# Indices and row weights on ScalarE, ranks ahead of splits, and another order at the end of an expert layer

## The chip, the cores and the metric

One core of a Trainium2 chip runs the whole program; there is no second core to wait for. The metric is the device time of one execution in microseconds (us), less is better. The engines run side by side, each through its own queue in order: TensorE (PE: matmuls, with weight loads listed apart as PEld), VectorE (DVE), ScalarE (ACT), GpSimd (POOL) and SyncE (SP), which here issues most of the DMA transfers. An instruction that waits holds back all that stands behind it on its engine.

## The reference

One decoder layer for 1024 tokens of width 1024:

```python
proj = x @ w_in + b_in                       # [q | k | v | u | g]
mix  = concat(attn(q, k, v), sgu(u, g)) @ w_out + b_out
h    = LN(alpha * x + mix)
y    = LN(alpha * h + MoE(h))
# MoE(h), top 4 of 32 experts for each token:
logits = h @ w_router + b_router
gates  = softmax(top_k(logits, 4))
gt  = minimum(rows @ w_gate[e] + b_gate[e], 7.0)
up  = clip(rows @ w_up[e] + b_up[e], -7.0, 7.0)
hid = gt * sigmoid(1.702 * gt) * (up + 1.0)
out = out.at[row_tok].add((hid @ w_down[e] + b_down[e]) * row_gate)
```

`rows` are the tokens that chose expert `e`, about 128 on average; each expert has three weight matrices of 1024 x 1024 in float32.

## The kernel before, in words

**Ahead of the experts.** Attention, gating, the output projection, the first layer norm and the router go block by block (eight blocks of 128 tokens). For each block `norm3a`/`norm3b` write `h`, split into two fp16 parts, to the table `htab` in DRAM, from which token rows are gathered later; they also write `h` to `h32` and `alpha * h` (scaled on GpSimd, L578) to the accumulator `acc`. `route1` to `route5` and their pieces (`route4a`, `route4p`, `route4g`) give each block its four experts, its gates and its place within each expert's list. The order of these calls, written out by hand for the last blocks, sets the order on every engine. The first two experts' token rows are found early: `places` makes one-hot rows, `rows` multiplies them with token numbers and gathers, and `early_g` and `weights_of` give those rows' gate weights from a tile `VE`.

**The expert loop.** `moe()` runs over 192 parts, called pieces: the two 512-column halves of gate ("g"), up ("u") and down ("d") of each of 32 experts. A piece is 96 matmuls (L1115): its 512 columns in four, 8 slices of the inner dimension, and three products of fp16 parts of weights and rows. The weights come as 1 MB halves into seven buffers `raw`. ScalarE makes the high fp16 part (`hi`, L948) and VectorE the low one (`lo`, L952), into one of three buffers `wsp`. So each piece costs two `hi` and two `lo`. Step `i` of the loop multiplies piece `i`, finishes piece `i-1` and splits the weights of piece `i+2`; the table `SEQ` gives the order within a step.

**The rows of an expert.** `rank` sorts the experts by load, in three parts between which other work is put (`next(rank)`); its result is the placement `PP` and a tile `V` with, for each token, its number and its gate weight for each slot. Expert slot `j` has a fixed room `CAP[j]` (88 to 256 rows; 48 groups of up to 128 rows for slots 2 to 31 and after). For each, events at fixed steps do `onehot` (VectorE, L1072), `rows_of` (TensorE, `V` times one-hot, L1082), `index` (one ScalarE copy, L932, and three GpSimd operations, L934 to L937, giving the token index `ix` and the weight `gw`), `gather` (GpSimd, indirect DMA `xg<-htab,ix`, L942), `xpose` (TensorE transposes, L1101) and `xcopy`. After the down pieces, `turn` transposes back and `combine` multiplies by `gw` (ScalarE) and adds to `acc` (indirect DMA).

**The end.** The eight blocks of `acc` are loaded back; the last expert's rows are added in SBUF apart. `FIN` says in which of the last steps each block's statistics (`s0` to `s7`, ScalarE and a power on GpSimd), its two passes (`a0` to `a7`, VectorE, L1327 and L1328, and a store L1329) and the last expert's end (`c1`, `c2`) are written. `c1` weights the last rows, adds, and takes their statistics with VectorE; `c2` normalizes and scatters them into the output, after all stores. `flags` checks all splits for numbers that are not finite and all experts for overflow. Every engine then reads that flag and skips a rescue path.

Of the kernel before, what the change touches and what calls it, by code (L numbers as in the profile page):

```python
# [20 lines left out]
EPS = 1e-5  # L21
# [10 lines left out]
FIN = {-3: ["s0", "s1", "a0"], -2: ["s2", "s3", "a1", "a2"], -1: ["s4", "s5", "a3", "a4"], 0: ["s6", "s7", "a5"],  # L32
       1: ["c1", "a6", "a7", "c2"]}
# [21 lines left out]
class Layer:  # L55
# [441 lines left out]
    def blocks(self):  # L497
# [112 lines left out]
        def route3a(b):  # L610
# [6 lines left out]
            gt = pb.tile([128, 44], F32, name="gt", bufs=2)  # L617
# [3 lines left out]
        def route3b(b):  # L621
# [4 lines left out]
            mr = pb.tile([128, 36], F32, name="mr", bufs=2)  # L626
# [39 lines left out]

        def early_g(b):
            sk = TK[b]
            for k in range(2):
                nc.vector.tensor_tensor(self.prod[:, k], sk[:, None, 32 + 32 * k:64 + 32 * k].to_broadcast([128, 2, NE]), self.SR,  # L670
                                        op=OP.mult)
            with nc.allow_low_precision(reason="one term of each sum differs from zero"):
                for k in range(2):
                    nc.vector.tensor_reduce(self.VE[:, b, :, 2 + k], self.prod[:, k], axis=AX.X, op=OP.add)
# [92 lines left out]
        norm3b(b - 1)  # L767
        self.loads(5)
# [3 lines left out]
        route1(b, (0,))  # L772
        norm3a(b)
        route1(b, (1,))
        route3b(b - 1)
        self.places(0, b - 2)
        route4p(b - 2)
        early_p(b - 2)
        route4g(b - 2)
# [3 lines left out]
        norm3b(b)  # L783
        route4p(b - 1)
        early_p(b - 1)
        self.places(b - 2, b)
        route3a(b)
        route3b(b)
        route4a(b)
        route4p(b)  # L790
# [4 lines left out]
        self.rows(1)  # L795
        self.loads()
# [120 lines left out]
    def weights_of(self):  # L917
        nc, p = self.nc, self.praw
        for j in range(2):
            self.rows_mm(j, 2)  # L920
# [678 lines left out]
```

## Time and profile before

| | |
|---|---|
| runs, us | 1731.23, 1731.42, 1733.17 (median 1731.42) |
| the profiled execution, us | 1732.75, its span 1731.0 |
| busy: PE | 1615.3 us (93%), 21936 instructions |
| busy: DVE | 1455.0 us (84%), 2128 |
| busy: ACT | 1184.8 us (68%), 1512 |
| busy: POOL | 509.4 us (29%), 437 |
| mean granted TensorE clock | 0.968 |

The span is the profiled part of one execution and its own time is 1.75 us longer. A busy share is a mean over stretches with different limits, so what an engine is worth is read for a stretch. In the rows below a timeline row is a start, a duration, the engine, the source line, the operation, what is written and what is read, its shape, and in brackets how long the engine stood idle before it and what released it. `x96` is a run of as many instructions. In the table of stretches each engine has its busy time and, behind it in brackets, its instructions; PEclk is the clock that TensorE was granted, as a share of full speed (2.4 GHz).

### The profile page before, as it was taken

How to read it: one execution, taken by the hardware profiler on the slowest of the kernel's cores; microseconds unless marked ns; L12 is line 12 of the kernel's file. 1: busy time of each engine (PE TensorE's matmuls, PEld its weight loads, DVE VectorE, ACT ScalarE, POOL GpSimd, SP SyncE). 2: the span in 40 equal slices, each digit the busy share in tenths (PEclk: the TensorE clock that was granted, in tenths of full speed). 3: DMA queues.
4: the chain of work that ended last, by engine and by line, in shares of the span. 5: the costliest groups of instructions: out<-in, count | busy, mean ns of one | idle time of the engine just before them, and what ended most of it. 6: DMA issues, size and time to landing. Idle time of an engine off the chain costs nothing. (4 is left out here: it accounts for less than half of the span.)

```text
span 1731.0 us, 51104 instructions
## 1 busy us (share of the span) xinstructions
PE 1615.3 (93%) x21936; PEld 1519.1 (88%) x21936; DVE 1455.0 (84%) x2128; ACT 1184.8 (68%) x1512; POOL 509.4 (29%) x437
## 2 busy tenths in 40 slices
PE   8989899946799999999999999999999999999981
PEld 7878666636799999999999999999999999999981
DVE  4555788898698898888898889898999989898886
ACT  4344455545677677777777777878787888777873
POOL 3310433332250712071215213222504142212013
PEclk9989999967899999999999999999999999999996
DMA  7331422279599998999999999999999999999993
GB/s 270 96 110 37 161 98 98 98 272 345 213 340 348 332 333 315 330 336 334 316 342 351 340 349 337 356 343 363 343 355 353 359 360 349 364 364 343 357 343 124
DMA packets 86713, 501.12 MB, mean 289 GB/s; under 512 B 14208, under 2 KB 14224, under 8 KB 37328
## 3 DMA queue, kind: packets, MB, share of 16 engines
q1 hardware_dynamic: 73632, 452.92, 69.8%
q0 software_dynamic: 12848, 44.86, 10.1%
q8 instruction: 174, 2.85, 0.6%
q14 instruction: 59, 0.48, 0.1%
HBM read 459.14 MB, written 38.60 MB: 288 GB/s over the span
## 5 line engine op out<-in xcount | busy, mean ns | idle before, releaser
L1115 PEld LDWEIGHTS <-wsp 128*128 128x128 f16 x18432 | 1161.1, 98 | 22.4 <-ACT xg L1323 6.5
L952 DVE SCALAR_TENSOR_TENSOR wsp<-raw,wsp 128x2048 f16<-128x2048 f32 x384 | 868.3, 2287 | 131.5 <-ACT wsp L948 129.7
L948 ACT ACTIVATE wsp<-raw 128x2048 f16<-128x2048 f32 x384 | 717.8, 1913 | 23.2 <-PE pu L1115 18.4
L1115 PE MATMUL pd<-hid,wsp 128*128 128x96 f16 (+30 forms) x6144 | 399.5, 227 | 10.2 <-ACT xg L1323 6.5
L1115 PE MATMUL pg<-xt,wsp 128*128 128x96 f16 (+30 forms) x6144 | 401.8, 227 | 0.0
L1115 PE MATMUL pu<-xt,wsp 128*128 128x96 f16 (+30 forms) x6144 | 398.7, 227 | 0.0
L1200 POOL DMA_INDIRECT acc<-y,ix x49 | 91.9, 1875 | 600.1 <-ACT y L1198 384.1
L934 POOL TENSOR_SCALAR ixf<-ixf,dummy 128x1 f32<-128x1 f32 (+7 forms) x48 | 118.1, 2461 | 272.1 <-ACT ixf L932 272.0
L1141 ACT ACTIVATE gv<-pg,bi 128x96 f32<-128x96 f32 (+30 forms) x256 | 79.9, 382 | 96.5 <-PE pg L1115 88.6
L942 POOL DMA_INDIRECT xg<-htab,ix x50 | 105.6, 2112 | 15.7 <-issue 12.1
L1198 ACT ACTIVATE y<-pt,gw 128x512 f32<-128x512 f32 (+7 forms) x98 | 62.0, 685 | 47.6 <-PE pt L1192 44.9
L1106 ACT COPY xt<-pt 128x1024 f16<-128x1024 f16 (+29 forms) x99 | 72.2, 783 | 31.0 <-PE pt L1101 15.8
L1169 ACT ACTIVATE hid<-uv 128x384 f16<-128x384 f32 (+28 forms) x102 | 47.7, 499 | 41.6 <-DVE uv L1166 41.6
L175 DVE TENSOR_TENSOR wl<-rw,wh 128x512 fp32r<-128x512 f32 x56 | 38.6, 737 | 40.7 <-ACT wh L174 40.7
L194 PE MATMUL psp<-xh,wh 128*128 128x512 f32 x160 | 65.4, 409 | 6.9 <-ACT xh L185 6.9
L195 PE MATMUL psp<-xl,wh 128*128 128x512 f32 x160 | 65.2, 407 | 3.8 <-DVE xl L187 3.7
L1101 PE MATMUL pt<-iden,xg 128*128 128x128 f16 (+29 forms) x800 | 46.2, 207 | 24.1 <-DMA xg<-htab,ix 16.7
L196 PE MATMUL psp<-xh,wl 128*128 128x512 f32 x160 | 64.4, 402 | 0.0
L1101 PEld LDWEIGHTS <-xg 128*128 128x128 f16 (+29 forms) x800 | 40.3, 99 | 26.4 <-DMA xg<-htab,ix 17.0
L523 PE MATMUL psp<-woh,mh 128*128 128x512 f32 x128 | 54.8, 428 | 3.5 <-issue 3.5
L1155 ACT ACTIVATE gv<-gv 128x384 f32<-128x384 f32 (+28 forms) x102 | 47.9, 515 | 11.4 <-DVE gv L1152 11.3
L1143 DVE SCALAR_TENSOR_TENSOR uv<-pu,bi 128x384 f32<-128x384 f32 (+28 forms) x102 | 53.7, 527 | 2.2 <-PE pu L1115 2.2
(278 smaller groups left out, 1746.5 us busy)
## 6 DMA issues: line engine op xcount, KB each, us to landing
raw<-w_g SPq DMA_DIRECT2D x128, 1024.0 KB, 7.7
raw<-w_u SPq DMA_DIRECT2D x128, 1024.0 KB, 7.4
raw<-w_d SPq DMA_DIRECT2D x128, 1024.0 KB, 7.1
rw<-w_t SPq DMA_DIRECT2D x20, 512.0 KB, 4.4
rw<-x_t SPq DMA_DIRECT2D x8, 512.0 KB, 4.6
rw<-w_m SPq DMA_DIRECT2D x8, 512.0 KB, 5.5
xb<-x SPq DMA_DIRECT2D x8, 512.0 KB, 4.3
htab<-t4k SPq DMA_DIRECT2D x8, 512.0 KB, 2.6
```

The source lines that it names most:

```text
L194: nc.tensor.matmul(pt, wh[:, k], xh[h, k], start=(k == 0), stop=False)
L195: nc.tensor.matmul(pt, wh[:, k], xl[h, k], start=False, stop=False)
L196: nc.tensor.matmul(pt, wl[:, k], xh[h, k], start=False, stop=(k == 7))
L934: v.tensor_scalar(t[:m, 0:1], t[:m, 1:2], self.dummy[:m, 1:2], t[:m, 0:1], op0=OP.mult, op1=OP.add)
L942: self.nc.gpsimd.indirect_dma_start(out=x[:m], out_offset=None, in_=self.htab, in_offset=bass.IndirectOffsetOnAxis(ap=self.IDX[j, o][:m], ...
L948: self.nc.scalar.activation(self.W[i][:, 0, 4 * z:4 * z + 4], self.RAW[i, z], AF.Copy, scale=WS)
L952: self.nc.vector.scalar_tensor_tensor(t[:, 1], self.RAW.pop((i, z)), WS, t[:, 0], op0=OP.mult, op1=OP.subtract, accum_out=self.FL[:, self. ...
L1101: nc.tensor.transpose(pt[:, k, :m], x[:m, z * D + 128 * k:z * D + 128 * k + 128], self.iden16[:m, :m])
L1106: (nc.vector.tensor_copy if j == 0 and z else nc.scalar.copy)(XT[j][:, z, :, o:o + m], XP.pop((j, o, z))[:, :, :m])
L1115: nc.tensor.matmul(out, w[:, wz, k, 128 * fc:128 * fc + 128], x[:, xz, k], start=(n == 0), stop=(n == 23))
L1141: nc.scalar.activation(out[:, q], src[:, q], AF.Identity, scale=1.0 / (HS * WS), bias=bi[:, c + q:c + q + 1])
L1200: nc.gpsimd.indirect_dma_start(out=self.acc, out_offset=bass.IndirectOffsetOnAxis(ap=IDX[j, o][:m], axis=0), in_=y[:m], in_offset=None, co ...
```

## The change

The change has five parts.

1. `index` no longer uses GpSimd: two ScalarE activations make the token index from the sums in PSUM, and a new `weight` makes the row weight with two more. Four ScalarE operations for a group take the place of one.
2. The two later parts of `rank` run at steps -4 and -1 instead of -1 and 1. For experts 2 and 3, `onehot` and `rows_of` run at steps 0 and 1, `index` and `gather` at 1 and 2, instead of steps 1 to 4 and 4 to 7.
3. `V` holds the token number and a one only once, the copies into it go from VectorE to ScalarE, `VE` and `early_g` are gone, and the row weights of the first two experts are made at step 4. Table constants come by a small DMA.
4. Ahead of the experts, `htab` is written first for the last two blocks, and `h32`, `alpha * h` (on ScalarE for these blocks) and `acc` follow later in `keep_h`; the first `hi` splits move up, the first `lo` splits into step -4.
5. At the end `FIN` has another order, the last statistics are made by ScalarE (`sums`), the flags stand after everything else, and the first half of the last down part goes through four slices of the inner dimension for both its groups before the other four.

```diff
-FIN = {-3: ["s0", "s1", "a0"], -2: ["s2", "s3", "a1", "a2"], -1: ["s4", "s5", "a3", "a4"], 0: ["s6", "s7", "a5"],
-       1: ["c1", "a6", "a7", "c2"]}
+FIN = {-3: ["s0", "s1"], -2: ["s2"], -1: ["s3", "a0", "a1"], 0: ["a2"],
+       1: ["c1", "s4", "s5", "a3", "s6", "a4", "c2", "s7", "a5", "a6", "a7", "c3"]}
...
+        def keep_h(b):
...
+            if b < NB - 2:
+                nc.gpsimd.tensor_scalar(ha, h, ALPHA, None, op0=OP.mult)
+            else:
+                nc.scalar.mul(ha, h, ALPHA)
             nc.sync.dma_start(self.acc[rows], ha)
...
         self.rows(1)
+        keep_h(b - 1)
+        self.loads(5)
+        keep_h(b)
+        self.hi(0, 1)
+        for z in range(2):
+            self.hi(1, z)
         self.loads()
         for i in (b - 2, b - 1, b):
-            if i > b - 2:
-                route4g(i)
-            early_g(i)
+            route4g(i)
             route5(i)
-        self.weights_of()
-        for z in range(2):
-            self.hi(0, z)
-            self.lo(0, z)
-            self.loads()
-        for z in range(2):
-            self.hi(1, z)
...
+    def weight(self, j, o, m, src):
         nc, p = self.nc, self.praw
+        t = p.tile([128, 4], F32, name="ixf", bufs=4)
+        nc.scalar.copy(t[:m, 2:3], src[:m, 2:3])
+        gw = self.GW[j, o] = p.tile([128, 1], F32, name="gw", bufs=16)
+        nc.scalar.activation(gw[:m], src[:m, 3:4], AF.Identity, scale=1.0 / G2S, bias=t[:m, 2:3])
 
     def index(self, j, o, m, src):
         nc, p = self.nc, self.praw
-        v = nc.gpsimd
         t = p.tile([128, 4], F32, name="ixf", bufs=4)
-        nc.scalar.copy(t[:m], src)
         ix = self.IDX[j, o] = p.tile([128, 1], I32, name="ix", bufs=16)
-        v.tensor_scalar(t[:m, 0:1], t[:m, 1:2], self.dummy[:m, 1:2], t[:m, 0:1], op0=OP.mult, op1=OP.add)
-        v.tensor_scalar(ix[:m], t[:m, 0:1], self.dummy[:m, 0:1], None, op0=OP.add)
-        gw = self.GW[j, o] = p.tile([128, 1], F32, name="gw", bufs=16)
-        v.tensor_scalar(gw[:m], t[:m, 3:4], 1.0 / G2S, t[:m, 2:3], op0=OP.mult, op1=OP.add)
+        nc.scalar.activation(t[:m, 0:1], src[:m, 0:1], AF.Identity, bias=self.dummy[:m, 0:1])
+        nc.scalar.activation(ix[:m], src[:m, 1:2], AF.Identity, scale=self.dummy[:m, 1:2], bias=t[:m, 0:1])
...
-                nc.vector.tensor_copy(self.V[:, 4 * g:4 * g + 4, :, 2 + i], pv[:, :, 32 + 32 * i:64 + 32 * i])
+                nc.scalar.copy(self.V[:, 4 * g:4 * g + 4, 1:, i], pv[:, :, 32 + 32 * i:64 + 32 * i])
...
-                for q in range(nf):
-                    mm(pt[:, q], w, x, f + q)
+                if (kind, j, hf) != ("d", NE - 1, 0):
+                    for q in range(nf):
+                        mm(pt[:, q], w, x, f + q)
+            if (kind, j, hf) == ("d", NE - 1, 0):
+                for q in range(2):
+                    for ks in ((0, 4), (4, 8)):
+                        for f, nf in groups(j):
+                            mm(PG[kind, j, hf, f][:, q], w, x, f + q, ks)
...
-                ev.setdefault((max(t - d, t0 + k), f.__name__), []).append((f, (j,)))
+                i = j - 2 + k // 2 if j < 4 else max(t - d, t0 + k)
+                ev.setdefault((i, f.__name__), []).append((f, (j,)))
...
-            if i in (-1, 1):
+            if i in (-4, -1):
                 next(rank, None)
+            if i == -4:
+                for z in range(2):
+                    lo(0, z)
+                    self.loads()
...
+            if i == 4:
+                for j in range(2):
+                    self.weights_of(j)
...
-            if i == n - 2:
-                self.flags(pmm)
...
+        self.flags(pmm)
```

On ScalarE, where the first gate part ends (`gv<-pg,bi` is its evacuation, `wsp<-raw` a `hi` split, `xt<-pt` a copy of transposed rows, `gv<-gv` the activation), there stood before:

```order
L948 ACTIVATE wsp_3261<-raw_3257 128x2048
L948 ACTIVATE wsp_3261<-raw_3258 128x2048
L1141 ACTIVATE gv<-pg,bi 128x88 x4
L1106 COPY xt_3660<-pt 128x768 x2
L948 ACTIVATE wsp_3152<-raw_3259 128x2048
L1155 ACT_TABLE_LOAD
L1155 ACTIVATE gv<-gv 128x352
```

and after, in the same place:

```order
L944 ACTIVATE wsp_3259<-raw_3256 128x2048
L932 ACTIVATE ixf<-pt,dummy 128x1
L933 ACTIVATE ix<-pt,ixf,dummy 128x1
L924 COPY ixf<-pt 128x1
L926 ACTIVATE gw<-pt,ixf 128x1
L932 ACTIVATE ixf<-pt,dummy 16x1
L933 ACTIVATE ix<-pt,ixf,dummy 16x1
L924 COPY ixf<-pt 16x1
L926 ACTIVATE gw<-pt,ixf 16x1
L1138 ACTIVATE gv<-pg,bi 128x88 x4
L1097 COPY xt_3679<-pt 128x768 x2
L944 ACTIVATE wsp_3152<-raw_3257 128x2048
```

The index and the row weights of expert 2 (two groups, 128 and 16 rows) now stand ahead of the evacuation of expert 0's gate part; before, the copies of expert 2's sums came behind that part's product.

On VectorE, at the start of the loop (`slot_e`, `slot_c`, `PP` and `V` are results of `rank`, `oh` the one-hot of expert 2, `wsp,FL<-raw` a `lo` split), there stood before:

```order
L952 SCALAR_TENSOR_TENSOR wsp_3261,FL<-raw_3258,wsp_3261 128x2048
L1039 CAST slot_e<-pt 1x32
L1041 COPY slot_c<-pt 1x32
L1051 CAST PP<-pt 128x128
L1053 CAST V<-pt 128x128 x2
L1051 CAST PP<-pt 128x128
L1053 CAST V<-pt 128x128 x2
L1152 TENSOR_SCALAR gv<-gv 128x352
L952 SCALAR_TENSOR_TENSOR wsp_3152,FL<-raw_3259,wsp_3152 128x2048
L952 SCALAR_TENSOR_TENSOR wsp_3152,FL<-raw_3148,wsp_3152 128x2048
L1072 TENSOR_TENSOR oh<-iota_79,PP 128x1152
```

and after:

```order
L1097 COPY xt_3491<-pt 128x704
L1031 CAST slot_e<-pt 1x32
L1033 COPY slot_c<-pt 1x32
L1040 CAST PP<-pt 128x128 x2
L948 SCALAR_TENSOR_TENSOR wsp_3258,FL<-raw_3150,wsp_3258 128x2048
L948 SCALAR_TENSOR_TENSOR wsp_3258,FL<-raw_3151,wsp_3258 128x2048
L948 SCALAR_TENSOR_TENSOR wsp_3259,FL<-raw_3255,wsp_3259 128x2048
L948 SCALAR_TENSOR_TENSOR wsp_3259,FL<-raw_3256,wsp_3259 128x2048
L1061 TENSOR_TENSOR oh<-iota_79,PP 128x1152
L1149 TENSOR_SCALAR gv<-gv 128x352
```

The last part of `rank` stands ahead of the four splits of pieces 1 and 2, and the one-hot of expert 2 ahead of the clamp of the first gate part and of the splits of piece 3; the copies of `V` are gone from VectorE.

On VectorE near the end (`yt<-pd,bi` evacuates a half of the last down part, `raw<-raw,fmv,xg` is one of a block's two passes, `bad` to `flag` are the flags), there stood before:

```order
L1327 SCALAR_TENSOR_TENSOR raw_3259<-raw_3259,fmv,xg_3262 128x1024
L1328 SCALAR_TENSOR_TENSOR raw_3259<-raw_3259,fmv,xg_3263 128x1024
L1335 TENSOR_SCALAR bad<-FL 128x384
L1336 TENSOR_SCALAR bad<-FH 128x8
L1338 TENSOR_REDUCE bads<-bad 128x1
L1342 TENSOR_SCALAR okf<-pt 128x1
...
L1348 CAST flag<-over 1x1
L1327 SCALAR_TENSOR_TENSOR raw_3259<-raw_3259,fmv,xg_3262 128x1024
L1328 SCALAR_TENSOR_TENSOR raw_3259<-raw_3259,fmv,xg_3263 128x1024
L1327 SCALAR_TENSOR_TENSOR raw_3148<-raw_3148,fmv,xg_3262 128x1024
L1328 SCALAR_TENSOR_TENSOR raw_3148<-raw_3148,fmv,xg_3263 128x1024
L1182 SCALAR_TENSOR_TENSOR yt<-pd,bi 128x2x124 x2
```

and after:

```order
L1179 SCALAR_TENSOR_TENSOR yt<-pd,bi 128x2x124 x2
L1334 SCALAR_TENSOR_TENSOR raw_3257<-raw_3257,fmv,xg_3260 128x1024
L1335 SCALAR_TENSOR_TENSOR raw_3257<-raw_3257,fmv,xg_3261 128x1024
L1334 SCALAR_TENSOR_TENSOR raw_3257<-raw_3257,fmv,xg_3260 128x1024
L1335 SCALAR_TENSOR_TENSOR raw_3257<-raw_3257,fmv,xg_3261 128x1024
L1179 SCALAR_TENSOR_TENSOR yt<-pd,bi 128x2x124 x2
L1334 SCALAR_TENSOR_TENSOR raw_3148<-raw_3148,fmv,xg_3260 128x1024
L1335 SCALAR_TENSOR_TENSOR raw_3148<-raw_3148,fmv,xg_3261 128x1024
L1210 TENSOR_TENSOR xg_3465<-xg_3465,y 128x512 x2
```

The first evacuation has no pass ahead of it, the second two instead of five, and the flags are gone from here to the end of the queue.

## Rows read from the trace of the kernel before

**Rows 1.** Stretches: length, PE, PEld, DVE, ACT, POOL busy, PEclk, DMA, GB/s.

```profile
390.00:500.00 110.00, 82.72 (x1532) 81.67 (x1531) 86.39 (x115) 68.06 (x85) 40.65 (x27) 0.85 0.78 291
...
560.00:1650.00 1090.00, 1085.69 (x16976) 1072.86 (x16974) 974.93 (x1190) 839.44 (x924) 319.62 (x233) 1.00 0.96 345
```

**Rows 2.** TensorE's timeline: start us, us, instruction, [idle before <- releaser].

```profile
409.76 0.62 PE L1082 MATMUL pt<-V,oh 128*128 128x4 f16 x16
...
414.40 3.92 PE L1115 MATMUL pg<-xt,wsp 128*128 128x88 f16 x96
...
429.58 1.89 PE L1101 MATMUL pt<-iden,xg 128*128 128x128 f16 x16 [11.25 <-DMA xg<-htab,ix]
...
431.25 5.34 PE L1115 MATMUL pu<-xt,wsp 128*128 128x88 f16 x96
```

**Rows 3.** GpSimd's timeline, 410 to 421 us.

```profile
410.68 3.44 POOL L934 TENSOR_SCALAR ixf<-ixf,dummy 128x1 f32<-128x1 f32 x1 [10.13 <-ACT ixf L932]
...
420.30 1.12 POOL L942 DMA_INDIRECT xg<-htab,ix  x1 [0.28 <-issue]
```

**Rows 4.** VectorE's waits, 384 to 530 us: us in total, times, longest us.

```profile
DVE wsp L952 <- ACT wsp L948: 22.8, 10, 13.5
```

**Rows 5.** VectorE's timeline, single rows from 289 to 441 us.

```profile
289.49 1.21 DVE L572 SCALAR_TENSOR_TENSOR t4k<-xb,t4k 128x1024 f16<-128x1024 f32 x1
...
359.25 2.04 DVE L572 SCALAR_TENSOR_TENSOR t4k<-xb,t4k 128x1024 f16<-128x1024 f32 x1
...
375.52 0.21 DVE L914 TENSOR_SCALAR ix<-ixf,dummy 96x1 int32<-96x1 f32 x1
...
381.23 0.22 DVE L679 COPY TS<-pst 96x128 f16<-96x128 f16 x1
...
382.90 0.22 DVE L679 COPY TS<-pst 96x128 f16<-96x128 f16 x1
...
384.43 2.28 DVE L952 SCALAR_TENSOR_TENSOR wsp<-raw,wsp 128x2048 f16<-128x2048 f32 x1
...
390.97 0.14 DVE L1033 CAST cnt<-pt 32x1 f16<-32x1 f32 x1
...
400.28 0.71 DVE L1053 CAST V<-pt 128x128 f16<-128x128 f32 x2
...
406.49 1.35 DVE L1072 TENSOR_TENSOR oh<-iota,PP 128x1152 f16<-128x1152 f16 x1
...
440.40 2.29 DVE L952 SCALAR_TENSOR_TENSOR wsp<-raw,wsp 128x2048 f16<-128x2048 f32 x1 [13.49 <-ACT wsp L948]
```

**Rows 6.** ScalarE's timeline, one row at 395 us and four near the end.

```profile
395.40 1.01 ACT L1141 ACTIVATE gv<-pg,bi 128x88 f32<-128x88 f32 x4 [5.91 <-PE pg L1115]
...
1682.86 1.04 ACT L1321 ACTIVATE xg<-raw 128x1024 f32<-128x1024 f32 x1
...
1685.53 1.06 ACT L1321 ACTIVATE xg<-raw 128x1024 f32<-128x1024 f32 x1
...
1702.85 0.20 ACT L1322 ACTIVATE fmv<-fmv 128x1 f32<-128x1 f32 x1
...
1704.25 1.26 ACT L1212 ACTIVATE y<-pt,gw 128x512 f32<-128x512 f32 x2
```

**Rows 7.** TensorE's timeline near the end.

```profile
1696.31 7.41 PE L1115 MATMUL pd<-hid,wsp 128*128 128x124 f16 x96 [6.48 <-ACT xg L1323]
```

**Rows 8.** VectorE's timeline near the end.

```profile
1713.73 1.28 DVE L1328 SCALAR_TENSOR_TENSOR raw<-raw,fmv,xg 128x1024 f32<-128x1024 f32 x1
```

**Rows 9.** The stretch of the flags, columns as in rows 1.

```profile
1688.55:1690.65 2.10, 0.18 (x1) 0.10 (x1) 1.69 (x10) 2.04 (x4) 0.70 (x2) 0.94 0.56 232
```

**Rows 10.** GpSimd's timeline near the end.

```profile
1711.62 2.34 POOL L1219 DMA_INDIRECT acc<-y,ix  x1 [0.18 <-issue]
...
1721.71 1.00 POOL L1229 DMA_INDIRECT out<-xg,ix  x1 [7.75 <-SPq L1355]
```

**Rows 11.** The stores of line 1329.

```profile
DMA to landing us min/median/max: 2.6/2.6/5.5
```

More of the change, by code (lines that the diff above doesn't have):

```diff
@@ L665, in early_p @@
             nc.vector.tensor_reduce(self.PE[:, b], self.prod[:, 0], axis=AX.X, op=OP.max)
[L667 to L674, printed above, removed]
         def route5(b):
@@ L775, in blocks @@
         route3b(b - 1)
[L776 to L779, printed above, removed]
+        self.hi(0, 0)
+        self.places(0, b - 1)
         route4a(b - 1)
@@ L782, in blocks @@
         route2b(b)
-        norm3b(b)
+        norm3b(b, False)
+        route3a(b)
+        route3b(b)
         route4p(b - 1)
         early_p(b - 1)
-        self.places(b - 2, b)
-        route3a(b)
-        route3b(b)
         route4a(b)
+        self.places(b - 1, b)
         route4p(b)
@@ L822, in open_raw @@
         self.SR = p.tile([128, 2, NE], F16, name="SR")
[L823 removed]
+        self.prod = p.tile([128, 1, 2, NE], F16, name="prod")
         self.FL = p.tile([128, NFL], F32, name="FL")
+        self.W, self.IDX, self.GW, self.XG = {}, {}, {}, {}
+        self.first = p.tile([1, NE], F32, name="first")
+        nc.sync.dma_start(self.first, self.a["caps"])
         self.nfl = 0
[L826 removed]
         pv = self.ps.tile([128, 512], F32, name="pst", bufs=2)
@@ L889, in ahead @@
             nc.vector.tensor_copy(self.PE[:, bs], v[:, :, 0:2])
-            for k in range(2):
-                nc.scalar.copy(self.VE[:, bs, :, 2 + k], v[:, :, 2 + 2 * k:4 + 2 * k])
     def places(self, b0, b1, js=(0, 1)):
@@ L1042, in rank @@
         self.over = p.tile([1, NE + 1], F32, name="over")
-        self.first = p.tile([1, NE], F32, name="first")
-        for j in range(NE):
-            nc.gpsimd.memset(self.first[:, j:j + 1], float(CAP[j]))
         nc.gpsimd.tensor_sub(self.over[:, 0:NE], self.slot_c, self.first)
@@ L1081, in rows_of @@
                 for b in range(NB):
-                    nc.tensor.matmul(p4[:m], oh[:, b, o:o + m], self.V[:, b, j], start=(b == 0), stop=(b == NB - 1))
+                    nc.tensor.matmul(p4[:m].rearrange("p (a c) -> p a c", c=2), oh[:, b, o:o + m], self.cols(b, j), start=(b == 0), stop=(b == NB - 1))
         def index(j):
             for o, m in subs(j):
-                self.index(j, o, whole(m), PT.pop((j, o))[:whole(m)])
+                src, m = PT.pop((j, o)), whole(m)
+                self.index(j, o, m, src)
+                self.weight(j, o, m, src)
         def gather(j):
@@ L1109, in moe, with mm @@
         OH, PT, PG = {}, {}, {}
-        def mm(out, w, x, fc):
-            n = 0
-            for k in range(8):
+        def mm(out, w, x, fc, ks=(0, 8)):
+            n = 3 * ks[0]
+            for k in range(*ks):
                 for wz, xz in ((0, 0), (0, 1), (1, 0)):
```

98 lines of the change are left out of this document (47 added, 51 removed).

## Prediction

> **What bounds the kernel now.** I read the page first, then a table of the span in stretches, the waits of TensorE and VectorE in the stretches that are not full, and last the timelines there. From 560 to 1650 us TensorE is busy 1085.7 of 1090 us at the full clock [rows 1]. Nothing that another engine does there can make the kernel shorter; there only a new TensorE wait can change the time. The time to be won lies in two places: the stretch from 375 to about 500 us, where the expert loop starts, and what follows the last multiply, from 1680 us on. From 390 to 500 TensorE is busy 82.7 of 110 us, at a mean granted clock of 0.85 [rows 1], and VectorE 86.4. The reader sees why on TensorE's timeline: at 418 us it has finished the piece that began at 414.40 and stands 11.25 us for `xg<-htab,ix`, the gathered rows of expert 2, which it must transpose before it goes on [rows 2]. GpSimd shows why they are late: it computes the token index only from 410.68 on (the first operation takes 3.44 us), and issues the gather at 420.30 [rows 3]; the transposes begin at 429.58, 9.3 us after that. VectorE meanwhile has no raw weights converted by ScalarE, since ScalarE's queue stands behind the same transposes: it waits 22.8 us in ten waits for `wsp`, the longest 13.5 [rows 4, 5]. In this stretch VectorE's queue, with two 2.3 us `lo` splits for each piece, is the pace, and its waits are what the stretch can lose.
>
> **Term 1, the first split earlier: 3.1 us.** Before, VectorE computes the last index of experts 0 and 1 at 375.52 and starts the first `lo` split at 384.43 [rows 5]: 8.7 us from the end of the one to the other. Between them lie gates of three blocks, the two `early_g` sums of each, the row weights of two experts, and a stalled cast. After, there remain three blocks and the first part of `rank`. The same line of two successive blocks stands at 381.23 and 382.90, so 1.67 us a block (its copy waits for TensorE's transpose, so that taking `early_g` out shortens it little): 5.0. `rank` takes 2.2 us: the two splits that begin at 384.43 end at 388.84 and its last VectorE row ends at 391.1. Together 7.2, a gain of 1.5. The `keep_h` work of blocks 6 and 7 moves from GpSimd ahead of this to ScalarE behind it. A subtract L572 takes 1.21 us where no GpSimd work runs beside it and 2.04 where GpSimd scales the same block [rows 5]; two of those lie on VectorE's way: 1.6 more. Sum 3.1; bounds 0 (TensorE and norm order, not VectorE, set the start) and 6 (the blocks shrink with `early_g`). By the Trainium skill, page "Advanced Engine Details and Errata", section Mode Summary, GpSimd and VectorE instructions that use VectorE's second port block each other; the two L572 rows agree, with 0.8 us between them. The page has no price for it; by the rule alone the 1.6 us stand, and the sum is the same.
>
> **Term 2, copies of V: 1.4 us.** Two VectorE rows L1053 of 0.7 us each go to ScalarE, which in this place waits for the first gate part anyway [rows 5]; the row at 395.40 has 5.91 us of idle time before it [rows 6]. On ScalarE they are hidden; without that cover they cost the same 1.4 there.
>
> **Term 3, the gathers of experts 2 and 3 no longer late: 21.7 us.** From the new start at 381.3 VectorE runs two splits (4.4), a copy and the last of `rank` (1.3), four splits (8.9), then the one-hot, 1.35 [rows 5]: its end is 397.3 instead of 407.8. TensorE's `rows_of` takes 0.62 [rows 2], the two index operations on ScalarE 0.2 each (the nearest is the 128x1 row of L1322 at 1702.85 [rows 6]) instead of two slow GpSimd ones, and the gather goes out near 398.5, not 420.3. With the same 9.3 us it is there at 407.8, and its transposes stand behind five pieces, which cannot end before 414 us even when none waits. So some 6 us are spare. Of VectorE's 22.8 us I count 21.7: the four waits over 1 us; the other six are the usual 0.2 between a `hi` and its `lo`.
>
> **Term 4, new stalls on ScalarE: minus 8.9 us.** What is moved now queues on ScalarE: for one expert of two groups eight small operations, 8 x 0.2 = 1.6 us, ahead of the gate evacuation L1141 in the same step, and they wait for `rows_of`, hence for VectorE's one-hot. VectorE's next row behind the one-hot is the clamp of that gate part. It stands for 0.62 + 1.6 + 1.01 (the evacuation at 395.40 [rows 6]) and the hand-overs, about 3.3. Expert 3's index stands ahead of the `hi` splits of the next pieces in the same way, and `lo` waits for these twice: 1.6 plus about one evacuation or its like, 1.2, is 2.8 each. 3.3 + 2.8 + 2.8 = 8.9. No row of before shows such a wait, so below it stands 0 (VectorE has a split left to run) and above 16 (the same again for experts 4 and 5). I take the middle, since VectorE's order leaves just one pair of splits between the two.
>
> **Term 5, TensorE at the lower clock: minus 2.8 us.** A part of 88 rows takes 3.92 or, behind a long wait, 5.34 us [rows 2]. The terms above use the short one; as the granted clock was 0.85 in the mean here, I charge two parts, 1.42 each; bounds 0 and 6. Elsewhere in the loop ScalarE gets some 0.6 us more per group and GpSimd loses its three operations; by [rows 1] ScalarE is busy 839 of 1090 us, so that is hidden by its idle quarter. Head: 3.1 + 1.4 + 21.7 - 8.9 - 2.8 = 14.5 us.
>
> **Term 6, the tail: 4.0 us.** Before, VectorE sets the end: passes and flags stand ahead of the evacuation that frees the last down part, which waits 6.48 us and then takes 7.41 [rows 7]; VectorE ends its last block's pass at 1715.0 [rows 8]. After, the evacuations come first, the last statistics go to ScalarE, and the flags (2.1 us [rows 9]) go last. Then ScalarE sets the pace: one statistics pass takes 2.67 us (1682.86 to 1685.53 [rows 6]); nine of them and the 1.26 of the weighting are 25.3, so 1708.2, and 1710.0 if the weighting waits for the last part. The last block's power on GpSimd stands behind the scatter into `acc` (its issue takes 2.34 us [rows 10]), then comes VectorE's second pass of 1.28: the end is 1710.5 to 1713.5, in the middle 1712, 3.0 earlier. The store behind it landed 5.5 us after its issue, others 2.6 [rows 11]; as the `acc` scatter now starts earlier than it did against this store, I take 1.0 less. GpSimd's scatter of the last rows, which waited 7.75 us for that store [rows 10], is 4.0 earlier. The last four half passes take 3 us and the flags 2.1, so their flag is ready near 1717.2, about when that scatter goes out: hidden, just. If not, they cost up to 2. Bounds 1.5 and 6.
>
> **Sum.** 14.5 + 4.0 = 18.5 us. The profiled execution took 1732.75 us (span 1731.0): 1714.25. The median of the runs, 1731.42, is 1.33 below it: **1712.9 us**.
>
> **Rivals.** *New stalls don't bite* (chance 0.13): VectorE has other splits to run while ScalarE does the indices. For it: before, `hi` runs ahead of `lo` almost everywhere. Against: three weight buffers only. Term 4 goes to 0, 1704.0. *ScalarE's order stalls again* (0.18): for experts 4 and 5, whose one-hots are wider, two or three more waits of 2.8: 5.6 to 8.4 lost, 1718.5 to 1721.3. For it: VectorE's slack is smallest where the weights have just started. Against: from 560 us on TensorE is never idle [rows 1], and the wide one-hots come late in this stretch. *The tail gives nothing* (0.12): the flags at the very end or the last block's power behind the scatter take what was won; 1716.9. *Slower* (0.05): ScalarE becomes what TensorE waits for in the whole loop. In each step the index goes ahead of the gate evacuation and holds it until `rows_of` is done; 48 groups with three more operations of 0.2 are 29 us, and if all of it held TensorE, the time would be 1712.9 + 29 = 1742. It decides from 0.6 us of wait for each of 30 experts, where the 18.5 are gone. For it: ScalarE runs in order. Against: TensorE's parts alternate between two accumulators of each kind, and ScalarE idles a quarter. The Trainium skill ("ScalarE: Activation LUTs", section What ACT_TABLE_LOAD costs) speaks for this rival: an activation with a per-partition bias takes about 280 ns even when small, so as an estimate three more of them are 0.84 us a group, 40 us over the loop and 1753 in all. The trace disagrees as far as its nearest row goes, the 128x1 activation of 0.20 us, and the measurement decides.
>
> **The numbers.** The forecast has 0.52, and its own spread is 1708 to 1718 by the bounds of terms 1, 5 and 6; with the rivals at 1704 and at up to 1721 the range is 1703 to 1722, which leaves out the slower case and the ends of the bounds. A measurement tells about 0.2%, 3.5 us, from no change. All cases but the last are faster by more than that; with some doubt that gains and stalls cancel, faster 0.93, the same 0.03, slower 0.04.
>
> **What would show it.** Right: the gather of expert 2 issued near 398 to 400 us, no TensorE wait for `xg` behind it, VectorE waits for `wsp` or `gv` of 2 to 4 us each, three of them; first `lo` split near 381; between 560 and 1650 nothing new; `rank` and splits in the new order with V's copies on ScalarE; the last part's wait gone and the last pass ending near 1712. Wrong: a TensorE wait of over 5 us for a gather or for ScalarE's `gv` in the head, ScalarE rows of 0.3 us and more for the index, a TensorE busy share under 99% in the loop, or flags after the last scatter.

## The result and the profile after

The changed kernel took 1714.26 us in the median of four runs (1713.50 to 1715.69), against 1731.33 for the kernel before in the same runs: a ratio of 0.9904, with an interval of 0.9892 to 0.9917. The forecast was 1712.9. The profiled execution took 1713.50, its span 1711.6. The two profiled executions lie 19.25 us apart and the medians 17.1, so the shares of the gain below, which come from the profiles, add up to 2 us more than the medians show.

Two points of time split the gain. The first statistics pass on ScalarE (L1321) starts right behind the last weight split, so all that comes before it is head and loop, and all behind it the end. It started at 1682.86 before [rows 6] and at 1667.14 after: 15.7 us from head and loop. From it to the end of the span were 48.2 us before and 44.5 after: 3.7 us from the end.

The stretches after; the columns are those of [rows 1]:

```profile
390.00:500.00 110.00, 91.80 (x1743) 90.30 (x1740) 95.52 (x119) 87.09 (x125) 10.52 (x9) 0.92 0.91 334
...
560.00:1640.00 1080.00, 1075.60 (x16748) 1062.60 (x16747) 964.87 (x1180) 859.30 (x1033) 160.68 (x109) 1.00 0.97 345
```

In the head TensorE is busy 9.1 us more within the same 110 us and its mean clock rose from 0.85 to 0.92; in the loop nothing changed for TensorE, and ScalarE carries some 28 us more (831.6 us before from 560 to 1640). TensorE's timeline in the head:

```profile
385.09 5.81 PE L1106 MATMUL pg<-xt,wsp 128*128 128x88 f16 x96
...
395.65 0.63 PE L1071 MATMUL pt<-V,oh 128*128 128x4 f16 x16 [4.75 <-DVE oh L1061]
...
398.79 5.81 PE L1106 MATMUL pu<-xt,wsp 128*128 128x88 f16 x96
...
409.46 0.64 PE L1071 MATMUL pt<-V,oh 128*128 128x4 f16 x16 [4.86 <-DVE oh L1061]
...
420.32 3.92 PE L1106 MATMUL pg<-xt,wsp 128*128 128x88 f16 x96
...
424.07 1.06 PE L1092 MATMUL pt<-iden,xg 128*128 128x128 f16 x16
```

The transposes of expert 2 (424.07) no longer wait, where before they stood 11.25 us [rows 2]; the gather went out on GpSimd at 397.72 instead of 420.30 [rows 3]:

```profile
397.72 0.97 POOL L938 DMA_INDIRECT xg<-htab,ix  x1 [12.84 <-ACT ixf L932]
```

TensorE now waits twice for the one-hot, 4.75 and 4.86 us; the `rows_of` behind each of these waits is what ScalarE then waits for. VectorE's waits between 370 and 530 us, as the total in us, their number, and the longest:

```profile
DVE wsp L948 <- ACT wsp L944: 10.7, 10, 3.0
...
DVE gv L1149 <- ACT gv L1138: 4.4, 2, 3.4
```

The waits for `wsp` were 22.8 us in ten [rows 4]. VectorE's own rows (the counterparts of [rows 5]) show when:

```profile
358.45 1.22 DVE L572 SCALAR_TENSOR_TENSOR t4k<-xb,t4k 128x1024 f16<-128x1024 f32 x1
...
365.48 1.21 DVE L572 SCALAR_TENSOR_TENSOR t4k<-xb,t4k 128x1024 f16<-128x1024 f32 x1
...
371.89 0.21 DVE L909 TENSOR_SCALAR ix<-ixf,dummy 96x1 int32<-96x1 f32 x1
...
379.37 2.27 DVE L948 SCALAR_TENSOR_TENSOR wsp<-raw,wsp 128x2048 f16<-128x2048 f32 x1
...
394.24 1.35 DVE L1061 TENSOR_TENSOR oh<-iota,PP 128x1152 f16<-128x1152 f16 x1
...
399.04 0.34 DVE L1149 TENSOR_SCALAR gv<-gv 128x352 f32<-128x352 f32 x1 [3.45 <-ACT gv L1138]
...
402.22 2.29 DVE L948 SCALAR_TENSOR_TENSOR wsp<-raw,wsp 128x2048 f16<-128x2048 f32 x1 [2.84 <-ACT wsp L944]
...
405.83 2.29 DVE L948 SCALAR_TENSOR_TENSOR wsp<-raw,wsp 128x2048 f16<-128x2048 f32 x1 [1.31 <-ACT wsp L944]
...
413.79 2.29 DVE L948 SCALAR_TENSOR_TENSOR wsp<-raw,wsp 128x2048 f16<-128x2048 f32 x1 [3.02 <-ACT wsp L944]
...
432.69 2.29 DVE L948 SCALAR_TENSOR_TENSOR wsp<-raw,wsp 128x2048 f16<-128x2048 f32 x1 [2.39 <-ACT wsp L944]
```

The first `lo` split starts at 379.37; the one-hot begins at 394.24, and behind it stand waits of 3.45, 2.84 and 1.31 us, then 3.02 behind the second one-hot, and 2.39. ScalarE, with V's four copies behind a wait at 385.19, shows what held it:

```profile
385.19 0.82 ACT L1042 CAST V<-pt 128x128 f16<-128x128 f32 x4 [2.33 <-DVE PP L1040]
...
396.32 0.26 ACT L932 ACTIVATE ixf<-pt,dummy 128x1 f32<-128x1 f32 x1 [6.75 <-PE pt L1071]
...
396.61 0.35 ACT L933 ACTIVATE ix<-pt,ixf,dummy 128x1 int32<-128x1 f32 x1
...
398.05 0.96 ACT L1138 ACTIVATE gv<-pg,bi 128x88 f32<-128x88 f32 x4
...
428.93 1.93 ACT L1097 COPY xt<-pt 128x1024 f16<-128x1024 f16 x2 [1.99 <-PE pu L1106]
```

From 396.32 to 398.05 run the eight small operations of expert 2, at 0.22 us each from start to start; but ScalarE had stood 6.75 us for `rows_of` before the first of them, with the gate evacuation (398.05) behind. The fifth wait, 2.39 us, is another matter: the `hi` split it waits for stands behind the copy of expert 2's transposed rows at 428.93, and ScalarE waits for TensorE there. Near the end the rows of TensorE, ScalarE, VectorE and GpSimd that answer to [rows 6 to 8] and [rows 10] are:

```profile
1670.36 5.39 PE L1106 MATMUL pd<-hid,wsp 128*128 128x124 f16 x96 [2.52 <-DVE yt L1179]
...
1667.14 1.04 ACT L1321 ACTIVATE xg<-raw 128x1024 f32<-128x1024 f32 x1
...
1694.46 1.28 DVE L1335 SCALAR_TENSOR_TENSOR raw<-raw,fmv,xg 128x1024 f32<-128x1024 f32 x1 [0.82 <-POOL fmv L1325]
...
1691.86 1.65 POOL L1215 DMA_INDIRECT acc<-y,ix  x1 [0.23 <-issue]
...
1700.45 1.05 POOL L1225 DMA_INDIRECT out<-xg,ix  x1 [6.03 <-DVE most L1353]
```

The last part waits 2.52 us instead of 6.48 and takes 5.39 instead of 7.41 (the granted clock in it is 1.00 instead of 0.71); the last pass ends at 1695.7, 28.6 us after the first statistics pass instead of 32.2.

### The profile page after: what moved, and what is told of

Its sections match the earlier page's. It is cut to its first block, busy times and chain, and to the rows that moved or that the text cites. A ratio compares the mean times of both kernels' runs of the same rounds, so it can differ in the third digit from the quotient of the medians.

```text
span 1711.6 us, 51003 instructions
## 1 busy us (share of the span) xinstructions
PE 1607.7 (94%) x21936; PEld 1511.0 (88%) x21936; DVE 1444.7 (84%) x2104; ACT 1222.9 (71%) x1667; POOL 303.1 (18%) x258
## 4 chain that ended last, share of the span: by engine, by line
PE 76%; DVE 8%; ACT 5%; issue 3%; DMA 0%; POOL 0%; DVEq 0%; ACTq 0%; POOLq 0%
PE pd L1106 21%; PE pu L1106 21%; PE pg L1106 21%; PE pt L1189 2%; PE pt L1092 2%; DVE wsp L948 2%; ACT wsp L944 2%; PE psp L523 1%; PE psp L525 1%; PE psp L524 1%; PE psc L370 1%; DVE s L403 1%; PE psp L194 1%; PE psp L195 1%; PE psp L196 1%
## 5 line engine op out<-in xcount | busy, mean ns | idle before, releaser
L1197 POOL DMA_INDIRECT acc<-y,ix x49 | 95.5, 1949 | 855.0 <-ACT y L1195 554.1
L938 POOL DMA_INDIRECT xg<-htab,ix x50 | 78.9, 1578 | 235.2 <-ACT ixf L924 208.2
L932 ACT ACTIVATE ixf<-pt,dummy 128x1 f32<-128x1 f32 (+7 forms) x48 | 12.0, 251 | 75.3 <-PE pt L1071 75.3
L1189 PE MATMUL pt<-iden,yt 128*128 128x128 f32 (+7 forms) x400 | 52.3, 273 | 3.0 <-POOL yt L1178 1.2
```

The costliest lines, as they stand in the source:

```text
L938: self.nc.gpsimd.indirect_dma_start(out=x[:m], out_offset=None, in_=self.htab, in_offset=bass.IndirectOffsetOnAxis(ap=self.IDX[j, o][:m], ...
L1189: nc.tensor.transpose(pt[:m, i], YT[j][:, 4 * g + i, o:o + m], self.iden)
L1197: nc.gpsimd.indirect_dma_start(out=self.acc, out_offset=bass.IndirectOffsetOnAxis(ap=IDX[j, o][:m], axis=0), in_=y[:m], in_offset=None, co ...
```

## The experiments

"Head" is the start of the first statistics pass, "end" the time from there to the end of the span, both of the one profiled execution; each ratio is to the kernel before run beside it on the same chip, not to the 1731.33 of the first row. Four of these kernels (after, e6, e10, e11) are the same program up to the last down part, and their profiles put the first statistics pass at 1667.1 to 1670.3: a difference of under 3 us in "head" is not told apart. "First `lo`" carries a spread too: the subtract that stands at 359.25 in [rows 5] starts between 358.3 and 360.4 in the twelve profiles, with the old head as with the new. The "end" of kernels with the same end agrees within 0.3 us but for two.

| kernel | median us | ratio, interval | first `lo` | head | end |
|---|---|---|---|---|---|
| before | 1731.33 | 1 | 384.4 | 1682.9 | 48.2 |
| after | 1714.26 | 0.9904 (0.9892 to 0.9917) | 379.4 | 1667.1 | 44.5 |
| e1_tail | 1727.16 | 0.9971 (0.9958 to 0.9984) | 383.7 | 1681.1 | 44.3 |
| e2_gpsimd_index | 1712.80 | 0.9882 (0.9867 to 0.9897) | 381.3 | 1667.6 | 44.5 |
| e3_scalar_index | 1713.62 | 0.9900 (0.9881 to 0.9918) | 385.4 | 1664.8 | 47.3 |
| e4_late_index | 1704.76 | 0.9842 (0.9828 to 0.9856) | 380.1 | 1657.5 | 44.5 |
| e5_double_small | 1720.07 | 0.9937 (0.9921 to 0.9953) | 379.4 | 1675.4 | 43.0 |
| e6_flags_early | 1715.26 | 0.9911 (0.9897 to 0.9924) | 379.5 | 1668.0 | 44.3 |
| e7_gpsimd_scale | 1715.48 | 0.9911 (0.9895 to 0.9927) | 382.4 | 1670.3 | 43.5 |
| e9_index_tail | 1711.99 | 0.9898 (0.9877 to 0.9919) | 385.6 | 1665.7 | 44.6 |
| e10_flags_old | 1717.68 | 0.9919 (0.9903 to 0.9936) | 379.7 | 1669.8 | 45.9 |
| e11_whole_last | 1714.93 | 0.9903 (0.9886 to 0.9919) | 380.2 | 1670.3 | 44.3 |

The theory: the gathers of experts 2 and 3 came too late, VectorE lost 21.7 us behind them, and anything that brings them in time wins this; ScalarE's place in the order decides what is given back. The rival: what wins is that slow GpSimd operations are gone, or that the whole order was moved.

**The end by itself** (before, with `FIN`, last statistics, last down part and flags as changed).

```diff
-FIN = {-3: ["s0", "s1", "a0"], ...
+FIN = {-3: ["s0", "s1"], -2: ["s2"], -1: ["s3", "a0", "a1"], 0: ["a2"],
+       1: ["c1", "s4", "s5", "a3", "s6", "a4", "c2", "s7", "a5", "a6", "a7", "c3"]}
...
```

> The kernel before with only the change at the end (FIN, flags last, last statistics on ScalarE, the last down part in quarters). Theory: head and tail add up, so the tail's own share of 3.7 us is seen alone, about 1727.6 us (ratio 0.998), with the last store issued about 28.6 us after the first statistics pass instead of 32.2. Rival: the flags at the very end cost what the rest wins, and the time stays within 1 us of before, 1731.

Its end is 44.3 us long, as in the changed kernel, its last pass 28.6 us after the first statistics pass, and its head that of before within the spread. So the end is worth 3.7 to 3.9 us here, with the old head as with the new; the median's 5.6 us below before (0.9971) has 3.7 in its interval.

**The index on GpSimd again, in the new order** (all other parts of the change stay).

```diff
-        nc.scalar.activation(t[:m, 0:1], src[:m, 0:1], AF.Identity, bias=self.dummy[:m, 0:1])
-        nc.scalar.activation(ix[:m], src[:m, 1:2], AF.Identity, scale=self.dummy[:m, 1:2], bias=t[:m, 0:1])
+        nc.scalar.copy(t[:m], src[:m])
+        v.tensor_scalar(t[:m, 0:1], t[:m, 1:2], self.dummy[:m, 1:2], t[:m, 0:1], op0=OP.mult, op1=OP.add)
...
```

> The changed kernel with the token index and row weight of experts 2 to 31 on GpSimd again, one ScalarE copy a group; the new order stays. Theory (what counts is that the gathers of experts 2 and 3 are there in time, and the order alone does that): rows_of ends near 396, GpSimd's operations take some 10 us, the gather goes out near 406 and is there near 415, before its transposes at 424; ScalarE has six small operations fewer ahead of the gate evacuation, so VectorE's new waits of 13 us shrink by 2 to 4. Time 1711 to 1715. Rival (the gain is GpSimd's slow operations taken away): 8 to 10 us lost, 1722 to 1725.

The first gather of expert 2 went out at 401.02 and was in time. VectorE's waits, two of its rows, and rows of GpSimd:

```profile
DVE wsp L952 <- ACT wsp L948: 10.8, 10, 3.0
...
DVE gv L1152 <- ACT gv L1141: 3.3, 3, 1.8
...
399.41 0.35 DVE L1152 TENSOR_SCALAR gv<-gv 128x352 f32<-128x352 f32 x1 [1.84 <-ACT gv L1141]
...
412.59 2.29 DVE L952 SCALAR_TENSOR_TENSOR wsp<-raw,wsp 128x2048 f16<-128x2048 f32 x1 [1.43 <-ACT wsp L948]
...
398.56 0.35 POOL L934 TENSOR_SCALAR ixf<-ixf,dummy 128x1 f32<-128x1 f32 x1 [11.71 <-ACT ixf L932]
...
401.02 1.05 POOL L942 DMA_INDIRECT xg<-htab,ix  x1 [0.46 <-issue]
...
412.68 4.46 POOL L937 TENSOR_SCALAR gw<-ixf 16x1 f32<-16x1 f32 x1
```

The head ended within 0.5 us of the changed kernel's. So the index need not be on ScalarE. One thing came otherwise than expected: GpSimd's six operations for expert 2 took 2.0 us and not 10, the first of them 0.35 us where it took 3.44 before [rows 3]. They are not slow by themselves. Before, a `lo` split of VectorE ran beside them; here VectorE stood waiting, and the one that met a split (412.68) took 4.46 us. In the kernel before, 47 of the 48 index operations of over 1.2 us overlap a `lo` split, and of the 81 that overlap none, all but one took 0.25 to 0.63. So this run did take the slow operations of expert 2 away. The rival falls all the same by an estimate from its rows: with the 7.3 us that they cost more before, the gather would go out near 408.3 and, with the 9.3 us to its transposes [rows 2, 3], be there near 417.6, ahead of those transposes at 425.36. What the order alone gives, without the other parts of the new head, was not run.

VectorE's new waits stay nearly as they were, 10.8 + 3.3 us against 10.7 + 4.4, with one ScalarE copy for a group instead of four operations. The waits right behind the two one-hots are 1.6 us shorter each (1.84 for 3.45, 1.43 for 3.02), but other waits of about 2 us came: in all the operations are worth 1 us of 15, where 2 to 4 were expected, and most of the waiting comes from `rows_of` in ScalarE's queue.

**The index on ScalarE, in the old order** (before, with `index` and `weight` of the changed kernel only).

> The kernel before with only the index and row weight on ScalarE; old order, old tail. Theory: the gather of expert 2 goes out near 411.5 instead of 420.3 and is there near 421, so that TensorE's wait of 11.25 us falls to 2 to 3 and expert 3's waits vanish; 12 to 17 us of the 21.7 are won by this alone, 1714 to 1719, so that order and engine each suffice for most of the gain and do not add. Rival (the order is what counts, and ScalarE in its old place only trades one wait for another): less than 6 us won, above 1725.

This alone brings the head 18.1 us down, a little more than the 12 to 17 expected, to 1664.8, below all four profiles of the changed head:

```profile
DVE wsp L955 <- ACT wsp L951: 5.6, 10, 2.5
...
412.34 0.98 POOL L945 DMA_INDIRECT xg<-htab,ix  x1 [10.83 <-DMA raw<-w_u]
...
411.42 0.26 ACT L939 ACTIVATE ixf<-pt,dummy 128x1 f32<-128x1 f32 x1 [0.70 <-PE pt L1085]
```

The gather went out at 412.34 and TensorE waited for no gather at all, where 2 to 3 us were expected; VectorE waited 5.6 us for `wsp`, and 2.5 of these are a wait at 528.86 that the other kernels have too, a little later. From the first `lo` split to the first statistics pass it is 19.1 us shorter than before. So the engine suffices, and so does the new head with the index on GpSimd; together they gain no more than the engine alone: where the old order has the index, `rows_of` is nearly done and ScalarE waits for it 0.7 us.

**The index and the end, in the old order.** Both of the edits above, nothing of the new head.

> The kernel before with the index and row weight on ScalarE and the new tail, everything at the head of the expert loop in its old order. Theory (ScalarE's index alone takes the gather stalls away, and the new order of one-hots and indices costs VectorE more waits than it takes): about 18 us from the index and 4 to 5 from the tail, 22 to 24 us below before, ratio 0.986 to 0.9875, faster than the whole change. Rival (the order ahead of the loop is part of the gain): at most as fast as the change, ratio 0.990 or more.

By its profile the two parts add: the head is 17.2 us down and the end 3.6. By the runs it is not told from the changed kernel (0.9898 with 0.9877 to 0.9919), so "faster than the whole change" was not shown. The new head, as the change has it, adds nothing that these runs can tell once the index is on ScalarE: it starts its first split 4 us sooner, counted from the first subtract, and loses that and more by VectorE's new waits.

**One step later.** The changed kernel, with `rows_of` of experts 2 and 3 one step, `index` and `gather` too one step behind where the change put them.

```diff
-                i = j - 2 + k // 2 if j < 4 else max(t - d, t0 + k)
+                i = j - 2 + min(k, 2) if j < 4 else max(t - d, t0 + k)
```

> The changed kernel with rows_of, index and gather of experts 2 and 3 one step later, so that ScalarE's index stands where rows_of has long been queued behind a part that ScalarE's next split must wait for anyway. Theory: the first three of VectorE's five new waits (3.45, 2.84, 1.31 us) and part of the next (3.02) go, the gathers go out near 406 and 416, land near 415 and 425 and are still in time; 5 to 8 us faster than the changed kernel, 1706 to 1709. Rival: TensorE at its lower clock takes up the time, or the gather is late by then: within 2 us of the changed kernel or slower.

It is the fastest version, 0.9842, its interval lies clear of the change's, and the gain over the change, 9.5 us in the medians, is more than the 5 to 8 expected. VectorE's waits, the head's stretch, expert 2's gather, and its index on ScalarE:

```profile
DVE wsp L948 <- ACT wsp L944: 6.3, 9, 2.5
...
DVE gv L1149 <- ACT gv L1138: 0.9, 1, 0.9
...
390.00:500.00 110.00, 101.98 (x1928) 100.75 (x1926) 106.26 (x133) 97.47 (x137) 13.08 (x9) 0.94 0.98 370
...
400.83 1.88 POOL L938 DMA_INDIRECT xg<-htab,ix  x1 [15.25 <-PE pg L1106]
...
399.44 0.24 ACT L932 ACTIVATE ixf<-pt,dummy 128x1 f32<-128x1 f32 x1
```

VectorE is busy 106.3 of the 110 us (95.5 in the changed kernel), so little is left to win from its waits there. Of the changed kernel's five waits two are left, 0.81 and 1.49 us; most of the rest of the 6.3 and 0.9 lies at 518 to 525 us, in waits that the changed kernel has behind 528. ScalarE's index now runs without any wait for `rows_of`. By the order of the program that product stands behind a part whose end ScalarE's next split needs in any case, since the part still reads the split's buffer.

**The small ScalarE operations twice.**

```diff
                 self.weight(j, o, m, src)
+                if j > 3:
+                    self.index(j, o, m, src)
+                    self.weight(j, o, m, src)
```

> The changed kernel with the four small ScalarE operations of index and row weight done twice for each group of experts 4 to 31 (the same values again). ScalarE gets some 45 us more of busy time in the loop. Theory (these operations lie in ScalarE's idle fifth, TensorE waits for none of them): within 2 us of the changed kernel, ratio to before 0.990 to 0.992. Rival (they hold the gate evacuation and so TensorE): 20 to 45 us slower, ratio above 1.0.

What came lies between the two. ScalarE was busy 1257.5 us instead of 1222.9, so 35 us more and not 45, and the head ends 5 to 8 us later than in the four profiles of the changed program; the ratios differ by 0.0033, 5.7 us. Rows of TensorE in the loop that have no wait in the changed kernel:

```profile
730.26 5.46 PE L1109 MATMUL pd<-hid,wsp 128*128 128x148 f16 x82 [0.82 <-DVE wsp L948]
...
736.50 0.63 PE L1071 MATMUL pt<-V,oh 128*128 128x4 f16 x16 [0.77 <-DVE oh L1061]
```

There are three such pairs between 550 and 950 us, 0.9 to 1.6 us each, in which TensorE is busy 3.9 us less than in the changed kernel. From the start of piece 40 to that of piece 188 the loop took 986.0 us, 5.4 more than the 980.6 of the changed kernel. At the single price the loop shows nothing: it took 980.1 before. So what the prediction called hidden by an idle quarter is hidden, but by a much smaller margin.

**GpSimd's scale back in its old place.** `keep_h` of the last two blocks called from `norm3b` again, with `nc.gpsimd.tensor_scalar`, and with it the stores of `h32` and `acc`.

> The changed kernel with h32, the scale by alpha and acc of the last two blocks written in their old place, the scale on GpSimd. Theory (GpSimd's work slows VectorE's subtract L572 beside it): the two subtracts take 2.0 us each again instead of 1.22, the first lo split starts 1.5 to 3 us later, and the time is 1 to 3 us above the changed kernel. Rival: the two durations had another cause, or the subtract is not on the way to the first split: within 1 us.

The first `lo` split came at 382.42, 2.3 to 3.1 us later than in the four profiles, but most of that is the spread ahead of the first subtract. From the start of this subtract to the first split it is 22.1 us, against 20.9 to 21.1 in the seven profiles of the new head and 25.2 in the four of the old one (before, e1, e3, e9): the scale on GpSimd costs 1.0 to 1.2 us. In the head's end and the ratio (0.9911 with 0.9895 to 0.9927) that is not told from the spread. VectorE's two subtracts, its first split, and GpSimd's two scales:

```profile
360.30 2.03 DVE L572 SCALAR_TENSOR_TENSOR t4k<-xb,t4k 128x1024 f16<-128x1024 f32 x1
...
368.31 1.22 DVE L572 SCALAR_TENSOR_TENSOR t4k<-xb,t4k 128x1024 f16<-128x1024 f32 x1
...
382.42 2.27 DVE L943 SCALAR_TENSOR_TENSOR wsp<-raw,wsp 128x2048 f16<-128x2048 f32 x1
...
360.22 2.78 POOL L583 TENSOR_SCALAR t4k<-xb 128x1024 f32<-128x1024 f32 x1
...
368.30 3.87 POOL L583 TENSOR_SCALAR t4k<-xb 128x1024 f32<-128x1024 f32 x1 [4.95 <-PE pst L603]
```

Only one subtract took 2.03, so the theory holds for half. For the other, the two engines began at the same moment, VectorE took 1.22 and GpSimd 3.87 instead of 2.78.

**The flags, and the last down part.** Ahead of the last pass; in their old place; and the last down part undivided.

```diff
-       1: [... "c2", "s7", "a5", "a6", "a7", "c3"]}
+       1: [... "c2", "s7", "a5", "a6", "f", "a7", "c3"]}
...
```

> The changed kernel with the flags ahead of the last block's pass instead of at the very end. Theory: VectorE stands idle there for 1.4 and 0.8 us, so the pass ends at most 1 us later; and the last scatter into the output, which took 5.6 us from issue to landing beside the instruction loads that all engines begin when the flag is out, takes 3.7 again as before: 1 to 2 us faster than the changed kernel, ratio 0.9894. Rival: the landing has another cause and VectorE's 2 us of flags come straight back: the same or 1 us slower.

The end is 44.3 us long: no gain, the outcome that the rival named. Both mechanisms are in it: the last scatter landed 4.1 us after its issue instead of 5.6, as the theory had it, and it went out 1.3 us later, behind the flags.

```diff
+            if i == n - 2:
+                self.flags(pmm)
...
-        self.flags(pmm)
```

> The changed kernel with the flags in their old place (step n - 2, between VectorE's passes), all else as changed; this shows what moving the flags is worth by itself. From the first statistics pass on, the last pass ended 28.6 us later in the changed kernel (32.2 before). Theory (ScalarE's chain sets the end there, VectorE has slack): the last pass ends within 1 us of 28.6 and the stretch from the first statistics pass to the end stays at 43 to 45 us; the flags' move alone is worth less than 1 us. Rival (VectorE's 2 us of flags were the gain): the stretch grows by 2 to 3 us, to 46.5 to 47.5.

What came lies between the two: the last pass ended 30.9 us after the first statistics pass instead of 28.6, and the end is 45.9 us long, 1.4 more. TensorE's last part and VectorE's last pass:

```profile
1675.19 7.00 PE L1106 MATMUL pd<-hid,wsp 128*128 128x124 f16 x96 [1.28 <-ACT xg L1324]
...
1699.33 1.28 DVE L1336 SCALAR_TENSOR_TENSOR raw<-raw,fmv,xg 128x1024 f32<-128x1024 f32 x1 [0.74 <-POOL fmv L1326]
```

The flags stand ahead of the evacuation. TensorE stands idle 1.90 and 1.28 us there, with one small matmul of the flags between, and then runs its part in 7.00 us instead of 5.39, at a granted clock of 0.76 instead of 1.00. So the flags' move is worth 1.4 of the 3.7 us, part of it through TensorE's clock.

> The changed kernel with the first half of the last down part in one piece per group again. Theory: TensorE does 12 matmuls instead of 24 ahead of its wait for the second half of hid and ends that part 0.7 to 1 us later, but VectorE evacuates it only after the last two lo splits, which end later still: no change, within 0.5 us in the stretch from the first statistics pass to the end. Rival: the evacuation, the second half, the weighting on ScalarE and all behind it move by 1 us or more.

As expected: 44.3 us, and the four-slice order of the last down part is worth nothing here.

## Why the prediction was right

**Term 1 (3.1 us forecast) was 4.2,** counted from the start of the first subtract, where the spread is out of it (25.2 us to the first split before, 20.9 after); the profile's 5.1 has 0.8 of that spread in it. What was said of the rows after held: 7.3 us from the last index to the first split (7.2 said), and both subtracts at 1.2. The rows before were misread in one place: between the last index and the first split stand the gates of two blocks and not of three. Those of the third ran at 366.70, ahead of the index; the change puts them behind it, and the index comes 1.0 us sooner. The stalled cast of the working is 3.4 of the 8.7 us by itself. It took 3.63 us, where the median of that line is 0.20, and ended as GpSimd had written the token numbers into `V`; the change writes them only once, in 0.21 us at 347.3. The two rows of the kernel before:

```profile
376.73 3.63 DVE L658 CAST sk<-gt 128x32 f16<-128x32 f32 x1
...
377.62 2.67 POOL L1010 IOTA V<- 128x256 f16 x1
```

With the scale on GpSimd 1.0 to 1.2 us of the term come back. That is the direction of the rule of the Trainium skill that the prediction weighed ("Advanced Engine Details and Errata", Mode Summary): the engines do hold each other up, and the run shows that either may be the one held.

**Term 2 (1.4) held** as far as the rows go: the copies of V run on ScalarE behind 2.3 us of idle time. No experiment has it alone.

**Term 3 (21.7) held,** and is the cause: the gather went out at 397.7 (398.5 said) and no gather is waited for. Two experiments bring it in time, one by the engine alone and one by the new head alone, and both win the head. The size without the new waits is 18.3 and 19.1 us from the first split on, in the two kernels that have the engine alone.

**Term 4 (minus 8.9) was minus 13.0,** the sum of the five waits above; 10.6 of it, the first four, come from the index. The first was right in size and in what it is made of, 3.45 us for 3.3: `rows_of`, eight operations, one evacuation. What the working left out is what follows: ScalarE, which has stood 6.75 us for a `rows_of` that stands behind VectorE's one-hot, makes its next two `hi` splits late too, and VectorE waits 2.84 and 1.31 us more. For expert 3 it counted two waits of 2.8, and one of 3.02 came. The duration of the small operations is the lesser part: with two copies in place of the eight, VectorE's waits shrank by 1 us in all. With the index one step later the standing is gone, and the head ends 9.6 us earlier.

**Term 5 (minus 2.8) did not show.** Parts of 5.81 us ran at 385.09 and 398.79, but each right before a TensorE wait for VectorE's one-hot, so they lay beside it. With the spread of the start, 5.1 + 1.4 + 21.7 - 13.0 = 15.2 against 15.7 in this profile (12.5 to 15.7 over the four): that the head's 14.5 was so nearly right is luck, since too small a gain, too small a loss and a loss that was none nearly cancel.

**Term 6 (4.0) was 3.7.** ScalarE's chain set the end, the last pass came 3.6 us earlier (3.0 said), and the last scatter went out 5.5 us earlier against the first statistics pass (4.0 said). Then 1.9 us came back that the working had named as the flags' price if they are not hidden: that scatter took longer to land. Before and after, in us from issue to landing, at the line's end:

```profile
out<-xg,ix POOLq DMA_INDIRECT x1, 3.7
```

```profile
out<-xg,ix POOLq DMA_INDIRECT x1, 5.6
```

With the flag ready earlier it was 4.1 and 4.0 (the two experiments on it). That the engines' loading of instructions after the flag takes the DMA queues from the scatter is argued from their packets in the same 2 us, and not shown.

**The rivals.** *New stalls don't bite* and *ScalarE's order stalls again* lie on either side of what came: 13.0 us of stalls, none of them for experts 4 and 5, where the second had them. *The tail gives nothing* falls with the first experiment. *Slower*, ScalarE as the bound of the loop, falls at the single price and shows its mechanism at the double one. The Trainium skill's price for a small activation with a per-partition bias, about 280 ns ("ScalarE: Activation LUTs", What ACT_TABLE_LOAD costs), was nearer than the 0.20 us row for one operation, 0.26 us here; in a row of eight they cost 0.22 each. Of the prediction's own signs, the three waits of 2 to 4 us were five, and one sign of being wrong came without harm, the index row of over 0.3 us (0.35).

## What to carry to other kernels

When a transfer is late, ask first by how much: two independent remedies for one wait do not add, and here either sufficed. Put an instruction that waits for another engine behind one that has to wait as long anyway, in the queue of the engine it is moved to; its own duration matters less than whom it holds. Spare time in a busy share is no licence: an engine idle for a fifth of a loop took 28 us for nothing and charged about 5 of the next 35. And before an operation is called slow, look at what runs beside it: the same GpSimd operation took 3.44 us beside a VectorE split and 0.35 where VectorE stood idle.

## What the runs showed of the hardware that was not expected

GpSimd and VectorE hold each other up, and either can be the one held. GpSimd's index operations on up to 128x1 took 0.25 to 0.63 us (one 1.36) where no `lo` split of VectorE ran, and up to 4.90 us beside one. A VectorE subtract took 2.03 us instead of 1.22 beside GpSimd's scale, the scale 3.87 instead of 2.78 when both began at the same moment, and a cast 3.63 instead of 0.20 beside GpSimd's iota. An activation on 128x1 took 0.26 us with one per-partition operand and 0.35 with two (this one also writes integers), a copy 0.15. The same indirect scatter of the last rows took 3.4 to 4.1 us to land in the four profiles whose flag is ready early, and 4.1 to 5.6 in seven whose engines read it right behind the issue; the cause is open.
